# Two unused strips in SBUF that shift the start of nearly every tile in a partition

## The chip, the cores and the metric

The kernel runs on one core of one Trainium2 chip. The metric is the device time of one execution in microseconds (us); less is better. TensorE does the matrix products, ScalarE (ACT) and VectorE (DVE) everything elementwise, and the tiles that they share lie in SBUF, a memory of 128 partitions. A tile has an address inside a partition, the same in all 128; that address is what this change is about.

## What is computed

The reference is a two-layer encoder trunk on x of 256 tokens x 1024 channels, in float32. Each layer is: half a SwiGLU feed-forward network (FFN), a token mixer, half an FFN; the first layer's mixer is a gated linear attention (GLA) in both directions, the second's a differential softmax attention.

```
def swiglu_ffn(h, w_gu, w_down):
    gate, up = jnp.split(h @ w_gu, 2, axis=-1)
    return (jax.nn.silu(gate) * up) @ w_down
...
for i in range(DEPTH):
    x = x + 0.5 * swiglu_ffn(rms_norm(x, norm_g[i, 0]), ffn_w_gu[i, 0], ffn_w_down[i, 0])
    h = rms_norm(x, norm_g[i, 1])
    x = x + (gla_mixer(h, ...) if i % 2 == 0 else diff_mixer(h, ...))
    x = x + 0.5 * swiglu_ffn(rms_norm(x, norm_g[i, 2]), ffn_w_gu[i, 1], ffn_w_down[i, 1])
```

w_gu is 1024 x 5632, w_down 2816 x 1024; there are four FFNs, so most of the products are theirs.

## The kernel before

**Weights.** `weight_plan` lists all weights in the order of use, in pieces of at most 1024 rows x 256 columns. Each piece is loaded into one of three `stage` buffers (8 KB of a partition), five pieces ahead, by DMAs on SP's queue (L119). ACT and DVE then split it into a high and a low part in float32r, the type that TensorE takes at one pass (L157, one of five `w` buffers of 16 KB). A float32 product is made of three float32r products: high.high, high.low, low.high.

**Products.** A matrix product takes a stationary operand of 128 x 128, which a LDWEIGHTS (engine PEld in the profile) puts into the array, and a moving operand, whose columns stream past it. Three helpers issue nearly all of them:

- `mm3` (L181, L182) in the gate and up halves of the FFN (tiles ps_g, ps_u) and in its down half (ps_d): for each 128-deep slice one product of 512 moving columns (both parts of the activations against the high weights), and one of 256 (high activations against the low weights). Stationary: w. Moving: the normalised x (x2, shown as x) in gate and up, the gated activations a2 (shown as a) in down.
- `mm1` (L174 to L176): three products of 256 columns each; stationary w. Moving: x2 for GLA's q, k and low-rank products, and the mixers' normalised outputs (o of GLA, do of the differential mixer) in `out_proj` (ps_w).
- `project_tok` (L196 to L198) and, in the last FFN, `down_out` (L388 to L390): three products of 256 columns each; stationary x2 or a2, moving w.

The small products of the mixers (scores, transposes, products with v) are in float32 or float32r on tiles of their own pools.

**Order.** The FFN runs over 11 pairs of column groups (gate, then up), then over 4 column groups of down in three pieces of depth each. The mixers follow an order written out by hand. All tiles come from pools, and the framework works out the waits; nothing in the source names an address.

**Addresses.** Pools lie one behind the other in the order in which they are opened, tiles inside a pool in the order in which they are first asked for, each on a multiple of 32 bytes. `const` comes first (the identity and the triangle `cst`, and small parameters), then `stage`, `wpool`, `xpool` (x and x2), `ev`, `small` (the statistics, some 50 tiles of 8 to 512 bytes), and behind it the pools that are opened for one stage at a time. All tiles of `stage`, `wpool`, `xpool` and of the stages' pools are whole multiples of 512 bytes, but for a few, so one remainder holds for a whole pool. In the program as built, the first byte of a tile, modulo 512, is:

| tiles | before | after |
|---|---|---|
| cst (identity, triangle) | 128 | 224 |
| stage, w, x, x2, acc, sq, half, rb | 416 | 0 |
| small statistics | all multiples of 32 | all multiples of 32 |
| a2, gate, up, sg, GLA's qk, v_tm, o2, w2, lr, the differential mixer's qkn, dv_tm, dT, o2 | 192 | 0 |
| qkd (GLA's decayed q and k) | 320 | 128 |

Every operand slice of a product begins a whole multiple of 512 bytes behind its tile's first byte, so it has its tile's remainder.

Of the kernel before, what the change touches and what calls it, by code (L numbers as in the profile page):

```python
# [11 lines left out]
F32 = mybir.dt.float32  # L12
# [6 lines left out]
P = 128  # L19
T = 256  # L20
# [17 lines left out]
# the differential mixer: h half a projection; for pair of heads p: bp statistics, np normalized q and k,  # L38
# sph scores and softmax of head h, fp the transposed probabilities, ap their products with v, op normalized; hold keeps weights
# from being split  # L40
# [3 lines left out]
# the gated linear attention: h half a projection; z the gate's logits, y its log decay, pi prefix sums of pair of  # L44
# heads i, ri its scores before decay, d l t the next level's decays, scores and place among the scores,
# ai products with v, gi output gate, oi normalized; hold keeps weights from being split, x lets them go
# [8 lines left out]
def weight_plan(w):  # L55
    """The weights in the order of use: [rows, columns] pieces of at most 1024 x 256, slices of rows, columns, copies."""
    plan = []

    def cols(a, start, width=CW, times=1):
        plan.append((a[:, start : start + width], KD, width, times))  # L60

    def ffn(i, j):
        gu, down = w["ffn_w_gu"][i, j], w["ffn_w_down"][i, j]
        for c in range(FF // CW):
            cols(gu, c * CW)
            cols(gu, FF + c * CW)
        for dc in range(D // CW):
            for k0 in range(0, NFB, KD):
                n = min(KD, NFB - k0)
                plan.append((down[k0 * P : (k0 + n) * P, dc * CW : (dc + 1) * CW], n, CW, 1))  # L70

    ffn(0, 0)
    gla = w["gla_w_in"][0]
    # four times side by side, to have the ranks on four groups of partitions
    cols(gla, gla.shape[1] - 32, 32, 4)
    for kind, c in GLA_COLS.split():
        cols(gla, {"q": 0, "k": 512, "v": 1024, "g": 2048}[kind] + int(c) * CW)
    for c in range(4):
        cols(w["gla_w_out"][0], c * CW)
    ffn(0, 1)  # L80
    ffn(1, 0)
    for kind, c in DIFF_COLS.split():
        cols(w["diff_w_in"][0], "qkv".index(kind) * D + int(c) * CW)
    for c in range(4):
        cols(w["diff_w_out"][0], c * CW)
    ffn(1, 1)
    return plan
# [3 lines left out]
def trunk(ctx: ExitStack, tc: tile.TileContext, ins, out):  # L91
# [3 lines left out]
    const = ctx.enter_context(tc.tile_pool(name="const", bufs=1))  # L95
    stage = ctx.enter_context(tc.tile_pool(name="stage", bufs=N_STAGE))
# [3 lines left out]
    small = ctx.enter_context(tc.tile_pool(name="small", bufs=2))  # L100
    psA = ctx.enter_context(tc.tile_pool(name="psA", bufs=6, space=bass.MemoryType.PSUM))
# [4 lines left out]
    plan = weight_plan(ins)  # L106
    staged, split = {}, {}
# [15 lines left out]
    def parts():  # L123
        """The parts of the next weights to split."""
        i = state["split"]
        _, nk, width, times = plan[i]
        t = staged.pop(i)
        w = split[i] = wpool.tile([P, KD, 2, CW], FR, tag="w", name=f"w{i}")
        state["split"] += 1
        step = 2 if i < 2 else 4  # L130
        for k0 in range(0, nk, step):
            ks = slice(k0, min(k0 + step, nk))
            whole, wh, wl = t[:, ks, :width], w[:, ks, 0, : times * width], w[:, ks, 1, : times * width]
            if times > 1:
                shape = [P, whole.shape[1], times, width]
                whole = whole[:, :, None, :].broadcast_to(shape)
                wh, wl = (z.rearrange("p k (c n) -> p k c n", c=times) for z in (wh, wl))
            high = partial(nc.scalar.activation, wh, whole, AF.Copy)
            low = partial(nc.vector.tensor_tensor, out=wl, in0=whole, in1=wh.bitcast(F32), op=ALU.subtract)
            yield high, low  # L140
# [10 lines left out]
    def issue(ops, after):  # L151
        """Each operation behind those of `after` that run on its engine."""
        with ExitStack() as order:
            for i in after:
                order.enter_context(tc.issue_after(i.ins))
            for op in ops:
                op()  # L157

    def release(*after):
        """The parts held back, behind `after`."""  # L160
        issue(held, after)
        held.clear()
        state["hold"] = None
# [8 lines left out]
    def mm1(ps, w, ms, act, k, first, last):  # L172
        """ps += wh.xh + wh.xl + wl.xh for one 128-deep slice."""
        mm(ps, lhsT=w[:, k, 0, ms], rhs=act[:, k, 0, :], start=first, stop=False)  # L174
        mm(ps, lhsT=w[:, k, 0, ms], rhs=act[:, k, 1, :], start=False, stop=False)  # L175
        mm(ps, lhsT=w[:, k, 1, ms], rhs=act[:, k, 0, :], start=False, stop=last)  # L176

    def mm3(ps, w, ms, act, k, first, last, wk=None):
        """ps[:, 0:256] += wh.xh + wl.xh, ps[:, 256:512] += wh.xl for one 128-deep slice."""
        wk = k if wk is None else wk  # L180
        mm(ps, lhsT=w[:, wk, 0, ms], rhs=act[:, k, :, :], start=first, stop=False)  # L181
        mm(ps[:, 0:T], lhsT=w[:, wk, 1, ms], rhs=act[:, k, 0, :], start=False, stop=last)  # L182
# [18 lines left out]
    def join(banks, out_t):  # L201
        """out = both halves of three-pass products."""
        h = ev.tile([P, 2, T], F32, tag="half", name="half")
        for b, ps in enumerate(banks):
            nc.scalar.copy(h[:, b, :], ps[:, T:512])  # L205
            nc.vector.tensor_tensor(out=out_t[:, b, :], in0=ps[:, 0:T], in1=h[:, b, :], op=ALU.add)  # L206

    def rsqrt(v, shape, name):
        """v ** -0.5 for v > 0."""
# [22 lines left out]
    # the tensor engine runs at half its clock until it has been busy for a while  # L232
# [18 lines left out]
    def load_gate(w2):  # L251
        """The second gate weights as rows of high, low, high, low parts, zero against the other direction's ranks."""
# [54 lines left out]
    def down(act, nk, coef, norm):  # L307
        """x += coef * act @ w, and the next norm's blocks as they come."""
# [26 lines left out]
    def out_proj(act, norm, parts, late):  # L335
        """x += act @ w; the two first column groups wait for `late` with their last slices."""
# [28 lines left out]
    def by_token(xt):  # L365
        """x with the tokens on the partitions."""
# [10 lines left out]
    def down_out(act, nk, coef, xt):  # L377
        """out = x + coef * act @ w, with the tokens on the partitions."""
# [18 lines left out]
    def first_norm():  # L397
        n = Norm(0)
        with ExitStack() as xctx:
# [8 lines left out]
            # neighbouring blocks lie in different banks, so that two engines can follow each other  # L408
# [73 lines left out]
    def gla(norm, nxt, w2):  # L482
        QK = KD // 2
        with ExitStack() as gctx:
# [7 lines left out]
            with tc.tile_pool(name="glb", bufs=2) as lp:  # L492
                # gate path: low rank -> log decay -> prefix sums per tile of 128 tokens
# [6 lines left out]
                # both directions' ranks, twice the high parts, twice the low ones  # L500
# [8 lines left out]
                def project_half(kind, c, n):  # L509
                    """Half a column group: of q and k half the columns, of v and g half the tokens."""  # L510
# [21 lines left out]
                # sums before each token, per pair of heads: forward's from column 0, backward's from column 1  # L532
# [5 lines left out]
                def gate_logits():  # L538
                    """z and exp(-|z|)."""
# [22 lines left out]
                def scores(q, k, name, cross=False):  # L562
                    """Scores^T [j, tile, head, i] of two heads."""
# [7 lines left out]
                def decay(hp, level):  # L571
                    """exp of the decays of queries and keys to the level's boundaries."""
# [14 lines left out]
                    if s == 1:  # L587
                        # the keys lie next to their boundary
# [130 lines left out]
    # relative-position bias by distance: frel[h, t] = table[bucket(t - 255), h]  # L719
# [14 lines left out]
    def diff(norm, nxt):  # L734
        with ExitStack() as octx:
            dp = octx.enter_context(tc.tile_pool(name="dif", bufs=1))
            # lambda
# [23 lines left out]
            def project_half(key, t, done):  # L761
                """Half the tokens of a column group; `done` takes the whole."""
                if t == 0:
                    half[key] = next_weights(), psA.tile([P, 2, CW], F32, tag="A", name="ps_d{}{}{}".format(*key))
                w, ps = half[key]
                project_tok(w, norm.x2, None, ps, (t,))
                if t == 1:
                    done(ps)
# [15 lines left out]
            def qk_stats(hp):  # L784
                # bias[q, k] with the queries in reverse: frel[h, k + (255 - q)]
# [4 lines left out]
                # mean square of q and k plus eps over the squared norm of x  # L790
# [24 lines left out]
            def softmax(hp, b):  # L815
# [22 lines left out]
                # p1 - lambda p2 times the sum of the first softmax, which the norm takes out again  # L838
# [28 lines left out]
            def attend(c):  # L867
                """Heads 2c and 2c + 1."""
# [31 lines left out]
            # halves of projections (h) between the steps of the pairs of heads  # L900
# [28 lines left out]
def constants():  # L929
    """What depends on the shapes alone."""  # L930
# [39 lines left out]
```

## Time and profile before

| | us |
|---|---|
| time, median of three runs | 1002.21 |
| lowest, highest run | 1001.0, 1005.1 |
| span of the profiled execution, first to last instruction | 1000.1 |
| PE busy in it | 994.5 |
| DVE, ACT busy in it | 748.0, 567.7 |

The profiled execution is one run with the hardware profiler; its span leaves out what lies before the first and behind the last instruction. A busy PE is not a PE at its best pace: a product counts as busy from its start to its modelled end, and products overlap. The pace is seen in the distance between the starts of two products.

### The profile page before, as it was taken

What the parts mean: (1) busy time and instruction counts of PE and PEld (TensorE: products, weight loads), DVE (VectorE), ACT (ScalarE), POOL (GpSimd) and SP (SyncE); (2) the same over time, 40 slices, a digit from 0 to 9 for tenths busy, and PEclk for the clock granted to TensorE, in tenths of its full rate; (3) what the DMA queues carried; (4) which work ended last, traced back from release to release, by engine and by line L of the source; (5) the groups of instructions that cost most, each with busy time, mean ns of one, the idle gap of its engine ahead of it and who ended that gap; (6) DMA issues with size and microseconds to landing.
All of it is one profiled execution on the core that took longest, in us unless ns stands there. A gap on an engine that the chain in (4) does not pass through costs nothing.

```text
span 1000.1 us, 16172 instructions
## 1 busy us (share of the span) xinstructions
PE 994.5 (99%) x6524; PEld 906.6 (91%) x6524; DVE 748.0 (75%) x1284; ACT 567.7 (57%) x962; POOL 2.0 (0%) x10
## 2 busy tenths in 40 slices
PE   9999999999999999999999999999999999999998
PEld 8888888999999888888888888889999998888998
DVE  6998756499877987774679787656989699767640
ACT  7666535397756755643456555435576577555430
POOL 0000000000000000000000000000000000000000
PEclk9999999999999999999999999999999999999999
DMA  9676544574322775545557555375655268555440
GB/s 295 221 263 209 190 158 135 194 226 154 127 85 85 256 248 178 190 159 187 167 176 248 195 184 178 128 240 171 194 149 169 65 200 274 178 171 193 158 132 22
DMA packets 176968, 178.95 MB, mean 179 GB/s; under 512 B 4419, under 2 KB 176222, under 8 KB 176894
## 3 DMA queue, kind: packets, MB, share of 16 engines
q1 hardware_dynamic: 176606, 177.68, 54.3%
q8 instruction: 51, 0.84, 0.3%
q10 hardware_dynamic: 256, 0.21, 0.1%
q14 instruction: 23, 0.19, 0.1%
q0 software_dynamic: 32, 0.02, 0.0%
HBM read 176.84 MB, written 1.06 MB: 178 GB/s over the span
## 4 chain that ended last, share of the span: by engine, by line
PE 98%; DVE 1%; DMA 0%; ACT 0%; issue 0%; ACTq 0%; POOLq 0%
PE ps_g L181 16%; PE ps_u L181 16%; PE ps_d L181 12%; PE ps_g L182 8%; PE ps_u L182 8%; PE ps_d L182 6%; PE ps_d L388 2%; PE ps_d L389 2%; PE ps_d L390 2%; PE ps_s L567 2%; PE ps_dqk L196 2%; PE ps_dqk L198 2%; PE ps_dqk L197 2%; PE ps_w L174 1%; PE ps_w L176 1%; PE ps_w L175 1%
## 5 line engine op out<-in xcount | busy, mean ns | idle before, releaser
L157 DVE TENSOR_TENSOR w<-stage,w 128x1024 fp32r<-128x1024 f32 x334 | 385.4, 1191 | 32.2 <-ACT w L157 31.9
L157 ACT ACTIVATE w<-stage 128x1024 fp32r<-128x1024 f32 x334 | 327.3, 1030 | 45.4 <-PE ps_d L390 17.0
L181 PE MATMUL ps_g<-x,w 128*128 128x512 f32 x704 | 249.3, 397 | 0.0
L181 PE MATMUL ps_u<-x,w 128*128 128x512 f32 x704 | 248.7, 395 | 0.0
L182 PE MATMUL ps_u<-x,w 128*128 128x256 f32 x704 | 197.5, 281 | 0.0
L182 PE MATMUL ps_g<-x,w 128*128 128x256 f32 x704 | 197.1, 281 | 0.0
L181 PE MATMUL ps_d<-a,w 128*128 128x512 f32 x528 | 183.2, 390 | 0.0
L181 PEld LDWEIGHTS ps_g<-x,w 128*128 128x128 f32 x704 | 132.0, 188 | 31.0 <-issue 0.9
L181 PEld LDWEIGHTS ps_u<-x,w 128*128 128x128 f32 x704 | 132.0, 188 | 30.7
L182 PE MATMUL ps_d<-a,w 128*128 128x256 f32 x528 | 149.0, 282 | 0.0
L182 PEld LDWEIGHTS ps_g<-x,w 128*128 128x128 f32 x704 | 133.4, 189 | 0.5
L182 PEld LDWEIGHTS ps_u<-x,w 128*128 128x128 f32 x704 | 133.1, 189 | 0.1
L181 PEld LDWEIGHTS ps_d<-a,w 128*128 128x128 f32 x528 | 99.1, 188 | 20.7
L182 PEld LDWEIGHTS ps_d<-a,w 128*128 128x128 f32 x528 | 99.9, 189 | 0.0
L276 ACT ACTIVATE x<-x,par 128x256 fp32r<-128x256 f32 x40 | 20.0, 507 | 117.5 <-DVE x L325 117.5
L205 ACT COPY half<-ps_u 128x256 f32<-128x256 f32 x88 | 32.7, 371 | 87.2 <-PE ps_u L182 85.4
L205 ACT COPY half<-ps_g 128x256 f32<-128x256 f32 x88 | 32.3, 370 | 83.5 <-PE ps_g L182 81.4
L206 DVE TENSOR_TENSOR up<-ps_u,half 128x256 f32<-128x256 f32 x88 | 36.9, 422 | 38.7 <-ACT half L205 38.6
L206 DVE TENSOR_TENSOR gate<-ps_g,half 128x256 f32<-128x256 f32 x88 | 36.8, 422 | 36.9 <-ACT half L205 36.9
L325 DVE SCALAR_TENSOR_TENSOR x<-ps_d,x 128x256 f32<-128x256 f32 x48 | 20.3, 424 | 57.9 <-PE ps_d L182 56.7
L388 PE MATMUL ps_d<-w,a 128*128 128x256 f32 x176 | 49.5, 281 | 0.0
L389 PE MATMUL ps_d<-w,a 128*128 128x256 f32 x176 | 49.5, 281 | 0.0
(232 smaller groups left out, 1560.6 us busy)
## 6 DMA issues: line engine op xcount, KB each, us to landing
stage<-in_ffn_w_gu_dram SPq DMA_DIRECT2D x86, 1024.0 KB, 5.1
stage<-in_ffn_w_down_dram SPq DMA_DIRECT2D x32, 1024.0 KB, 4.8
stage<-in_ffn_w_down_dram SPq DMA_DIRECT2D x16, 768.0 KB, 4.1
stage<-in_gla_w_in_dram SPq DMA_DIRECT2D x12, 1024.0 KB, 5.6
stage<-in_diff_w_in_dram SPq DMA_DIRECT2D x12, 1024.0 KB, 5.5
stage<-in_gla_w_out_dram SPq DMA_DIRECT2D x4, 1024.0 KB
stage<-in_diff_w_out_dram SPq DMA_DIRECT2D x4, 1024.0 KB, 4.9
stage<-in_ffn_w_gu_dram SPq DMA_DIRECT2D x8, 256.0 KB, 5.7
```

Of the source, the lines that this page charges most:

```text
L157: op()
L181: mm(ps, lhsT=w[:, wk, 0, ms], rhs=act[:, k, :, :], start=first, stop=False)
L182: mm(ps[:, 0:T], lhsT=w[:, wk, 1, ms], rhs=act[:, k, 0, :], start=False, stop=last)
L196: mm(ps[:, t, :], lhsT=act[:, k, 0, ts_], rhs=w[:, k, 0, :], start=k == 0, stop=False)
L197: mm(ps[:, t, :], lhsT=act[:, k, 0, ts_], rhs=w[:, k, 1, :], start=False, stop=False)
L198: mm(ps[:, t, :], lhsT=act[:, k, 1, ts_], rhs=w[:, k, 0, :], start=False, stop=k == KD - 1)
L205: nc.scalar.copy(h[:, b, :], ps[:, T:512])
L206: nc.vector.tensor_tensor(out=out_t[:, b, :], in0=ps[:, 0:T], in1=h[:, b, :], op=ALU.add)
L325: nc.vector.scalar_tensor_tensor(out=x[:, d, :], in0=ps[:, h * T : (h + 1) * T], scalar=coef, in1=x[:, d, :], op0=ALU.mult, op1=ALU.add,)
L388: mm(ps, lhsT=act[:, k0 + k, 0, ts_], rhs=w[:, k, 0, :], start=first, stop=False)
L389: mm(ps, lhsT=act[:, k0 + k, 0, ts_], rhs=w[:, k, 1, :], start=False, stop=False)
L390: mm(ps, lhsT=act[:, k0 + k, 1, ts_], rhs=w[:, k, 0, :], start=False, stop=last)
```

## The change

Two tiles are asked for that nothing writes or reads: 96 bytes of each partition at the front of `const`, and 224 bytes at the end of what `small` has asked for at that point. They shift what lies behind them; the table above has both states. Nothing else changes but comments and docstrings, which are gone: with the line numbers left out, the built program has the same instructions on the same engines in the same order, with the same waits, row for row. Lines behind L95 stand three lines further down in the changed kernel (L181 becomes L184).

```
     const = ctx.enter_context(tc.tile_pool(name="const", bufs=1))
+
+    const.tile([P, 24], F32, name="gap0")
     stage = ctx.enter_context(tc.tile_pool(name="stage", bufs=N_STAGE))
     wpool = ctx.enter_context(tc.tile_pool(name="wpool", bufs=N_W))
     xpool = ctx.enter_context(tc.tile_pool(name="xpool", bufs=1))
     ev = ctx.enter_context(tc.tile_pool(name="ev", bufs=2))
     small = ctx.enter_context(tc.tile_pool(name="small", bufs=2))
+    small.tile([P, 56], F32, tag="gap", name="gap1", bufs=1)
     psA = ctx.enter_context(tc.tile_pool(name="psA", bufs=6, space=bass.MemoryType.PSUM))
```

The 224 bytes bring the stages' pools, and the 96 bytes those ahead of `small`, to multiples of 512.

## Rows read from the trace of the kernel before

**Rows 1.** Page: busy us of each engine; granted TensorE clock; the chain by engine.
```profile
PE 994.5 (99%) x6524; PEld 906.6 (91%) x6524; DVE 748.0 (75%) x1284; ACT 567.7 (57%) x962; POOL 2.0 (0%) x10
...
PEclk9999999999999999999999999999999999999999
...
PE 98%; DVE 1%; DMA 0%; ACT 0%; issue 0%; ACTq 0%; POOLq 0%
```

**Rows 2.** Groups by line: count, busy us, mean ns of one, idle before.
```profile
L181 PE MATMUL ps_g<-x,w 128*128 128x512 f32 x704 | 249.3, 397 | 0.0
...
L181 PE MATMUL ps_d<-a,w 128*128 128x512 f32 x528 | 183.2, 390 | 0.0
...
L388 PE MATMUL ps_d<-w,a 128*128 128x256 f32 x176 | 49.5, 281 | 0.0
...
L196 PE MATMUL ps_dqk<-w,x 128*128 128x256 f32 x128 | 36.6, 286 | 0.0
```

**Rows 3.** PE in order of time, first FFN's gate and up, 60 to 80: first, last of 117.
```profile
59.68 0.39 PE L181 MATMUL ps_g<-x,w 128*128 128x512 f32 x1
...
79.79 0.39 PE L181 MATMUL ps_g<-x,w 128*128 128x512 f32 x1
```

**Rows 4.** As rows 3, second FFN's gate and up, 400 to 420: first, last of 115.
```profile
399.79 0.28 PE L182 MATMUL ps_g<-x,w 128*128 128x256 f32 x1
...
419.93 0.28 PE L182 MATMUL ps_u<-x,w 128*128 128x256 f32 x1
```

**Rows 5.** Stretches: busy us of PE (instructions), granted clock, DMA share, GB/s.
```profile
550.00:570.00 20.00, 20.00 (x117) 1.00 0.60 200
840.00:860.00 20.00, 20.00 (x115) 1.00 0.71 236
```

**Rows 6.** As rows 3, second FFN's down, 460 to 480: first, last of 117.
```profile
459.68 0.39 PE L181 MATMUL ps_d<-a,w 128*128 128x512 f32 x1
...
479.79 0.39 PE L181 MATMUL ps_d<-a,w 128*128 128x512 f32 x1
```

**Rows 7.** As rows 3, differential mixer's q and k, 697 to 712: first, last of 128.
```profile
696.74 0.28 PE L196 MATMUL ps_dqk<-w,x 128*128 128x256 f32 x1
...
711.98 0.28 PE L197 MATMUL ps_dqk<-w,x 128*128 128x256 f32 x1
```

**Rows 8.** As rows 3, GLA's output projection, 306 to 319: first, last of 113.
```profile
305.82 0.28 PE L175 MATMUL ps_w<-o,w 128*128 128x256 f32 x1
...
318.89 0.28 PE L176 MATMUL ps_w<-o,w 128*128 128x256 f32 x1
```

**Rows 9.** As rows 3, last FFN's down, 950 to 970: first, last of 172.
```profile
949.75 0.28 PE L390 MATMUL ps_d<-w,a 128*128 128x256 f32 x1
...
969.99 0.28 PE L390 MATMUL ps_d<-w,a 128*128 128x256 f32 x1
```

**Rows 10.** Pieces of the chain: start us, us, what (mixers' small products).
```profile
202.41 0.92 PE ps_z L543 x4
...
289.27 0.43 PE ps_av L635 x2
...
785.76 1.80 PE ps_do L874 x16
```

**Rows 11.** Groups by line and shape: DVE and ACT at 512 elements.
```profile
L472 DVE TENSOR_TENSOR a<-up,a 128x512 fp32r<-128x512 f32 x44 | 30.2, 686 | 0.8 <-ACT a L471 0.7
L471 ACT ACTIVATE a<-up 128x512 fp32r<-128x512 f32 x44 | 27.5, 624 | 2.2 <-DVE up L469 2.1
...
L157 DVE TENSOR_TENSOR w<-stage,w 128x512 fp32r<-128x512 f32 x18 | 12.2, 685 | 0.0
...
L157 ACT ACTIVATE w<-stage 128x512 fp32r<-128x512 f32 x18 | 11.0, 616 | 0.0
```

**Rows 12.** Page: DMA queue of the weights; SP's longest wait by line.
```profile
q1 hardware_dynamic: 176606, 177.68, 54.3%
...
SPq L119 <- DVE w L157: 783.0, 153, 19.4
```

More of the change, by code (lines that the diff above doesn't have):

```diff
@@ L95, in trunk @@
     const = ctx.enter_context(tc.tile_pool(name="const", bufs=1))
+    const.tile([P, 24], F32, name="gap0")
     stage = ctx.enter_context(tc.tile_pool(name="stage", bufs=N_STAGE))
@@ L100, in trunk @@
     small = ctx.enter_context(tc.tile_pool(name="small", bufs=2))
+    small.tile([P, 56], F32, tag="gap", name="gap1", bufs=1)
     psA = ctx.enter_context(tc.tile_pool(name="psA", bufs=6, space=bass.MemoryType.PSUM))
```

## The prediction

> **What bounds the kernel now.** I read the page first. [...] The groups of PE show no idle time ahead of them [rows 2]. So there is no wait to shorten: the time is the sum of the distances between the starts of 6524 products, and a change moves it through that pace or hardly at all. I therefore took the timeline of PE in stretches where one pattern repeats, and divided: (start of the last row - start of the first) / steps between them. A "pair" is one product of 512 and one of 256 moving columns of `mm3`.
>
> - First FFN, gate and up: 59.68 to 79.79 in 116 steps, 58 pairs: 346.7 ns a pair [rows 3].
> - Second FFN, the same code on the same addresses modulo 512: 399.79 to 419.93 in 57 pairs: 353.3 ns [rows 4]. The third FFN has 117 rows in 20 us as the first, the fourth 115 as the second [rows 5].
> - Down: 459.68 to 479.79 in 58 pairs: 346.7 ns [rows 6].
> - Differential mixer's q and k, 256 columns each: 15.24 us in 127 steps: 120.0 ns [rows 7].
> - GLA's output projection, 256 columns each: 13.07 us in 112 steps: 116.7 ns [rows 8].
> - Last FFN's down, 256 columns each: 20.24 us in 171 steps: 118.4 ns [rows 9].
>
> The reader is to see two things. The pace has two levels that differ by 2 to 3%: quick (346.7, 116.7) and slow (353.3, 120.0). And the level goes with the remainders of the two operands. Written as (moving, stationary): (416, 416) gives 120.0 at 256 columns, and either 346.7 or 353.3 in pairs; (192, 416) gives 116.7 and 346.7; (416, 192) gives 118.4. 416 is an odd multiple of 32, 192 is a multiple of 64. The slow pace is at its fullest where both operands begin at an odd multiple of 32, and it is absent where the moving one does not.
>
> **The change part by part.** It adds no instruction and no wait and takes none away; the order on each engine is the same. What can change is the duration of what reads and writes the shifted tiles.
>
> *DVE and ACT.* The same shape at two remainders: at 512 elements DVE takes 686 ns on tiles at 192 and 685 ns on tiles at 416, ACT 624 and 616 [rows 11]. No price of the remainder shows up to multiples of 64, so I take 0. If something smaller came of it, PE's idle column of 0.0 covers it [rows 2]: neither engine is waited for in the steady stretches.
>
> *DMA.* The weights' rows now land at 0 instead of 416. Their queue keeps the 16 engines busy for 54.3% of the span, and SP's queue spends 783.0 us waiting for DVE to free a stage buffer [rows 12], so a load that ends sooner only waits longer. I take 0. The one load that PE itself waits for is in the first 10 us, worth some tenths of a us either way.
>
> *Transposes.* cst goes from 128 to 224, an odd multiple of 32. It is the moving operand of the transposes and of GLA's prefix sums, 160 instructions. At the 3.3 ns that separate the two paces of 256 columns this is 0.5 us at most (no row has cst elsewhere): 0 to +0.5, and I take 0.
>
> *The products.* Now every large operand pair is (0, 0). I take for it the quick pace, since 0 is a multiple of 64, as 192 is:
> (a) gate and up of the FFNs that run slow. The second and the fourth do [rows 4, 5]; each has 11 x 2 x 16 = 352 pairs (ps_g and ps_u have 704 products of 512 columns each over four FFNs [rows 2]): 2 x 352 x 6.6 ns = 4.7 us.
> (b) 256 columns at (416, 416): L196 to L198 with 128 + 64 + 64 + 64 products each, L174 to L176 with 72 each that have x2 as moving operand: 3 x (320 + 72) = 1176, x 3.3 ns = 3.9 us.
> (c) the last down: 3 x 176 = 528 [rows 2], x 1.7 ns = 0.9 us.
> (d) down (1056 products) and the output projections (384) are at the quick pace already: 0.
> The sum is 9.5 us. The profiled span of 1000.1 becomes 990.6. The median of the runs is 2.1 us above that span, so 992.7, rounded to **993**.
>
> The bounds of (a) to (d) from other rows: no gain at all, if the remainder has nothing to do with the pace; and the paces of the small float32 products as a floor. Those run at 112 ns with 128 columns (1.80 us for 16), and at 216 ns with one float32 pass over 256 (0.43 us for 2) [rows 10], which I take as the nearest rows for 256 and 512 float32r columns. They give the third rival below.
>
> [...]
>
> **The rivals.**
>
> *The remainder does nothing.* The two paces would be states into which the stream of products falls at the start of a stretch, and the mixers' difference would come from what precedes them. For it: the first and the second FFN have the same remainders and different paces, so the remainder alone doesn't decide. Against it: q, k, v, g and the differential mixer's q, k, v come to 120.0 after every interruption, some 30 times, and the output projections to 116.7 to 118 each time. Time: 1002.2, with 352 x 6.6 ns = 2.3 us for each gate-and-up stage that changes its state: 998 to 1007. The three runs of before lie 4.1 us apart, about two such steps.
>
> *Slower: equal remainders are what is slow.* The rows allow the other reading: (416, 416) is slow because the two are equal, so that the two streams of reads keep step, and (192, 416) and (416, 192) are quicker because they differ. After the change all are equal. Down may fall to the slow pace, 528 x 6.6 = 3.5 us; the output projections 384 x 3.3 = 1.3; the last down 528 x 1.6 = 0.8: +5.6 us, 1007.8. If the quick gate-and-up stages go slow as well, +4.7 more, 1012.5; if down stays quick, 1004.3. What decides is whether down after the change runs at 346.7 or 353.3. For it: four float32r products of GLA's gate, 512 columns at (192, 192), take 0.92 us, 230 each [rows 10], no quicker than the 512-column products of the FFN; so being at multiples of 64 on both sides gives nothing beyond the quick pace, and perhaps not even that. Against it: in the first FFN (416, 416) runs at 346.7.
> [...]
>
> *Larger gain.* Even the quick pace is above the floor: 346.7 against 216 + 112 = 328. If a start at a multiple of 128 or 512, which no large operand of before has, removes that too, the pairs give 18.7 ns on 704 + 528, and 25.3 on 704: 23.0 + 17.8; 256 columns give 8.0 on 1176, 4.7 on 384 and 6.4 on 528: 9.4 + 1.8 + 3.4. In all 55 us: 947; half of it: 974. For it: nothing in the trace excludes it. Against it: the pace is the same 346.7 at 416 and at 192, where some difference would be expected, and GLA's 230 ns.
>
> **How the numbers follow.** Quick pace everywhere 0.36 (its own range 988 to 998), the remainder does nothing 0.30, equal remainders 0.20, larger gain 0.14. A difference of 0.5%, 5 us, is about what a measurement of this kernel can tell from none: 997.2 and 1007.2 are the bounds. Faster: 0.31 + 0.14 + 0.01 = 0.46. Slower: 0.15 of the equal remainders and 0.02 of the stages' states: 0.17. Same: 0.37. The range goes up to the middle of the equal remainders, 1008, and down to a little beyond half the larger gain, 970; outside are about 0.06 above and 0.10 below.
>
> **What would show it.** In the changed kernel's timeline: 346.7 ns a pair in all four gate-and-up stages (117 rows in 20 us, never 115); 116.7 instead of 120.0 in the differential mixer's q and k; 116.7 in the last down; down and output projections unchanged. Mean durations of L181 with x as moving operand would be near 390 ns as those of down are, not 397 [rows 2]. It is wrong if q and k stay at 120.0 (the remainder does nothing, or equality is what counts), if down or the output projections slow down (equality), or if any pair goes below 340 ns (larger gain).

## The result: slower, and the profile after

| | before | after |
|---|---|---|
| median, us (6 runs each) | 1002.88 | 1010.41 |
| lowest, highest | 1000.46, 1005.1 | 1008.87, 1011.04 |
| span of the profiled execution | 1000.1 | 1008.6 |

The ratio of after to before is 1.0079, with a 95% interval of 1.0063 to 1.0094: about 8 us slower, where 993 us had been forecast, outside the range of 970 to 1008.

The page of the changed kernel has the same shape as that of before [rows 1]; PE is still the bound, and its busy time has grown with the span:

```profile
PE 1003.1 (99%) x6524; PEld 908.2 (90%) x6524; DVE 748.4 (74%) x1284; ACT 568.3 (56%) x962; POOL 2.0 (0%) x10
...
PEclk9999999999999999999999999999999999999999
```

DVE and ACT moved by 0.4 and 0.6 us, the granted clock not at all (9 in all 40 slices of both pages). In the groups by line (mean ns of one behind the busy time) the product that has changed most is the one that was to stay as it was: the 512-column product of down, 390 ns before [rows 2], has 399 now, as gate has.

```profile
L184 PE MATMUL ps_g<-x,w 128*128 128x512 f32 x704 | 251.0, 399 | 0.0
...
L184 PE MATMUL ps_d<-a,w 128*128 128x512 f32 x528 | 186.7, 399 | 0.0
```

The timeline of PE, in the second FFN's down (465 to 485, 115 rows), GLA's output projection (311 to 323, 103 rows) and the last FFN's down (960 to 980, 169 rows), first and last row of each:

```profile
464.77 0.28 PE L185 MATMUL ps_d<-a,w 128*128 128x256 f32 x1
...
484.91 0.28 PE L185 MATMUL ps_d<-a,w 128*128 128x256 f32 x1
```

```profile
310.75 0.28 PE L179 MATMUL ps_w<-o,w 128*128 128x256 f32 x1
...
322.99 0.29 PE L179 MATMUL ps_w<-o,w 128*128 128x256 f32 x1
```

```profile
959.81 0.28 PE L391 MATMUL ps_d<-w,a 128*128 128x256 f32 x1
...
979.97 0.28 PE L391 MATMUL ps_d<-w,a 128*128 128x256 f32 x1
```

The time from the first start to the last, divided by the steps between them: 20.14 us in 57 pairs, 353.3 ns (before 346.7 [rows 6]); 12.24 us in 102 steps, 120.0 ns (116.7 [rows 8]); 20.16 us in 168 steps, 120.0 ns (118.4 [rows 9]). The differential mixer's q and k stay at 120.0 [rows 7]. In gate and up, stretches of 20 us (and one of 16) show 115 products where the pace is 353.3 and 117 where it is 346.7:

```profile
60.00:80.00 20.00, 20.00 (x115) 1.00 0.79 256
...
560.00:580.00 20.00, 20.00 (x115) 1.00 0.54 177
840.00:860.00 20.00, 20.00 (x115) 1.00 0.80 261
914.00:930.00 16.00, 16.00 (x94) 1.00 0.54 178
```

The third FFN and, from 45 us on, the first, both quick before [rows 3, 5], are slow now. The fourth begins slow, as before, but from its interruption by the transposes of x on (895 to 899 us) it is quick: 353.3 from 828 to 895 us, 346.7 from 899 us on (94 in 16 us).

The 8.5 us of the span can be given to stages: the first product of each stage starts, in the two timelines, at these times.

| stage | start before | start after | longer by |
|---|---|---|---|
| first FFN, gate and up | 8.96 | 8.89 | 1.75 |
| down | 134.21 | 135.89 | 1.17 |
| GLA | 195.23 | 198.08 | 0.55 |
| second FFN, gate and up | 319.71 | 323.11 | 0.10 |
| down | 444.77 | 448.27 | 1.17 |
| third FFN, gate and up | 505.79 | 510.46 | 2.13 |
| down | 628.82 | 635.62 | 1.17 |
| differential mixer | 689.84 | 697.81 | 0.40 |
| fourth FFN, gate and up | 807.16 | 815.53 | -0.80 |
| last down | 934.25 | 941.82 | 0.9 |

Of the last column (a stage's length after less its length before) the three downs make 3.5 us, gate and up 3.2, the two mixers 0.95, the last down 0.9. No stage of any length became quicker but a part of the fourth gate and up. The last down's 0.9 counts to the end of the span.

### The profile page after: what moved, and what is told of

The parts are those of the page before. It is cut to its first block, busy times and chain, and to the rows that moved or that the text cites. A ratio compares the mean times of both kernels' runs of the same rounds, so it can differ in the third digit from the quotient of the medians.

```text
span 1008.6 us, 16172 instructions
## 1 busy us (share of the span) xinstructions
PE 1003.1 (99%) x6524; PEld 908.2 (90%) x6524; DVE 748.4 (74%) x1284; ACT 568.3 (56%) x962; POOL 2.0 (0%) x10
## 3 DMA queue, kind: packets, MB, share of 16 engines
q1 hardware_dynamic: 176606, 177.68, 53.3%
## 4 chain that ended last, share of the span: by engine, by line
PE 98%; DVE 1%; DMA 0%; ACT 0%; issue 0%; ACTq 0%; POOLq 0%
PE ps_g L184 16%; PE ps_u L184 16%; PE ps_d L184 12%; PE ps_g L185 8%; PE ps_u L185 8%; PE ps_d L185 6%; PE ps_d L393 2%; PE ps_d L392 2%; PE ps_d L391 2%; PE ps_s L570 2%; PE ps_dqk L199 2%; PE ps_dqk L201 2%; PE ps_dqk L200 2%; PE ps_w L177 1%; PE ps_w L178 1%; PE ps_w L179 1%
## 5 line engine op out<-in xcount | busy, mean ns | idle before, releaser
L184 PE MATMUL ps_g<-x,w 128*128 128x512 f32 x704 | 251.0, 399 | 0.0
L184 PE MATMUL ps_u<-x,w 128*128 128x512 f32 x704 | 250.2, 398 | 0.0
L184 PE MATMUL ps_d<-a,w 128*128 128x512 f32 x528 | 186.7, 399 | 0.0
L184 PEld LDWEIGHTS ps_g<-x,w 128*128 128x128 f32 x704 | 132.3, 188 | 32.5 <-issue 0.9
L184 PEld LDWEIGHTS ps_u<-x,w 128*128 128x128 f32 x704 | 132.1, 188 | 32.1
L184 PEld LDWEIGHTS ps_d<-a,w 128*128 128x128 f32 x528 | 99.2, 188 | 24.7
```

## The experiments

The theory after the result: the pace of a stream of products hangs on the **distance** of its two operands, the moving one's address less the stationary one's, and not on where each begins. Theory E below is its first form (equal remainders are what is slow), theory D its later one (only the distance modulo 256 bytes counts). The rival: it hangs on each operand's own remainder (theory O). All kernels below are the kernel before with strips in up to three places: `gap0` at the front of `const` (shifts everything behind it), `gapx` at the front of `xpool` (shifts x, x2 and what follows against w), `gap1` at the front of `small` (shifts the statistics and the stages' pools). Nothing else differs: the same instructions in the same order. Ratios are to the kernel before, run on the same chip.

**One strip alone.**

```
+    const.tile([P, 24], F32, name="gap0")
```

> Only the 96 bytes in const: w and x2 at 0 (equal), a2 and the mixers' outputs at 288, so that the distance of moving and stationary operand is that of before in every product. Theory E (equal remainders of the two operands are what is slow): down 346.7 ns a pair, output projections 116.7, last down 118.4, q and k of the differential mixer 120.0; time as before, 1000 to 1005. Theory O (an operand's own remainder counts; 0 and odd multiples of 32 are slow, 192 is quick): 288 is an odd multiple of 32, so down 353.3, output projections 120, as in the changed kernel; 1008 to 1011.

```
+    small.tile([P, 56], F32, tag="gap", name="gap1", bufs=1)
```

> Only 224 bytes in small: w and x2 stay at 416, a2 and the mixers' outputs come to 416 too, all equal but not at 0. Theory E: as the changed kernel: down 353.3 ns a pair, output projections 120, last down 120; 1007 to 1012. Theory O with 0 as what is slow: nothing is at 0, down stays at 346.7 and the time at 1000 to 1005. Theory O with odd multiples of 32 as what is slow: as theory E.

Measured: with the first strip alone 1005.03 us (1002.97 to 1006.49), ratio 1.0019 [1.0004, 1.0033]; with the second alone 1012.38 us (two runs, 1011.89 and 1012.86), ratio 1.0094 [1.0065, 1.0123]. The times lie a little above theory E's ranges, on a chip where the kernel before has a median of 1003.35. Second FFN's gate and up and its down, first with the first strip alone, then with the second alone (busy us, products, clock, DMA):

```profile
410.00:430.00 20.00, 20.00 (x115) 1.00 0.47 154
465.00:485.00 20.00, 20.00 (x117) 1.00 0.46 156
```

```profile
410.00:430.00 20.00, 20.00 (x115) 1.00 0.60 196
465.00:485.00 20.00, 20.00 (x115) 1.00 0.45 145
```

With w and x2 at 0 and a2 at 288, down is at 346.7 ns a pair (20.11 us in 58 pairs) as before; with everything at 416, it is at 353.3 (20.14 in 57) as in the changed kernel. So 0 is not what is slow (it is absent in the second kernel), and an odd multiple of 32 is not either (288 is one, and is quick): theory O falls in both its forms. The second strip makes the loss; the first is worth 0.2% (0.0 to 0.3), and its profiled span is 1.0 us longer than that of the kernel before (1001.1 and 1000.1). What the second strip does to down, the output projections and the last down follows from the distance of a2 and the mixers' outputs to w. With it the first and third FFN's gate and up are at 353.3 too, as in the changed kernel, though their own distance is 0 with the strip and without it; why is open.

**Other distances: 64 and 32, 256 and 128.**

```
+    const.tile([P, 24], F32, name="gap0")
...
+    xpool.tile([P, 64], F32, tag="gapx", name="gapx")
...
+    small.tile([P, 24], F32, tag="gap", name="gap1", bufs=1)
```

> w at 0, x2 at 256, a2 and the mixers' outputs at 128. Theory E with 512 as the modulus: no pair of operands is equal, so all pairs at 346.7 ns, 256 columns at 116.7 to 118.4; 994 to 998. With 256 as the modulus: x2 and w count as equal, gate and up, q and k as in the changed kernel (353.3, 120), down and the output projections quick; 1000 to 1006. With 128 or less: all slow, 1008 to 1011. Theory O with 0 modulo 128 as what is slow: all slow, 1008 to 1011.

```
+    const.tile([P, 24], F32, name="gap0")
...
+    xpool.tile([P, 16], F32, tag="gapx", name="gapx")
...
+    small.tile([P, 48], F32, tag="gap", name="gap1", bufs=1)
```

> w at 0, x2 at 64, a2 and the mixers' outputs at 32. Theory E with a modulus of 128 or more: no pair is equal, all pairs at 346.7 ns; 994 to 998. With 64 as the modulus: gate and up, q and k as in the changed kernel, down and the output projections quick; 1000 to 1006. With 32: all slow, 1008 to 1011. Theory O (0 and odd multiples of 32 slow): all slow but x2; 1004 to 1011.

Measured: 1007.26 us (three runs, 1007.04 to 1009.54), ratio 1.0045 [1.0019, 1.0072], and 1003.04 us (1000.41 to 1005.33), ratio 0.9998 [0.9979, 1.0016]. First the second FFN's gate and up with x2 256 away from w, then its down with a2 32 away:

```profile
410.00:430.00 20.00, 20.00 (x115) 1.00 0.59 196
```

```profile
465.00:485.00 20.00, 20.00 (x117) 1.00 0.63 209
```

With x2 256 away from w, gate and up of the first, second and third FFN are at 353.3 (115 products from 60 to 80, 410 to 430 and 560 to 580 us), and the fourth's at 346.7 (117 from 840 to 860): the two paces that equal remainders have. With a2 at distance 32, down is at 346.7, the output projection at 116.7 and the last down at 118.4: what the kernel before has at distance 288. So 256 counts as 0 here and 288 as 32; theory D takes the distance modulo 256 from these two. Neither theory had what the other distances gave; for the two kernels theory E, with a modulus of 256, had 1000 to 1006 and 994 to 998. At 128 down has a pace between the two (e3, 465 to 485, 57 pairs in 20.01 us: 351.1 ns), and at 64 gate and up are at 353.3 in some stretches (115 rows from 410 to 430, 560 to 580 and 840 to 860 us) and at 348.9 in the last stretch of the fourth (93 rows from 914 to 930 us). Quick or slow is not one switch: 351.1 and 348.9 lie between 346.7 and 353.3.

**The remaining distances.**

```
+    const.tile([P, 24], F32, name="gap0")
...
+    xpool.tile([P, 24], F32, tag="gapx", name="gapx")
...
+    small.tile([P, 80], F32, tag="gap", name="gap1", bufs=1)
```

> w at 0, x2 at 96, a2 and the mixers' outputs at 192: distances not seen yet. Theory D fixes what was seen: the last down has distance -192, that is 64, so 117.4 ns as GLA's q and k had at 64; output projections at 192, so 114 to 116 as the differential mixer's q and k had there. New: pairs at 96 and 192, 256 columns at 96 and 160; between 346 and 353 and between 114 and 120. Theory O or a modulus of 512 gives no reason why the last down should be at 117.4.

```
+    const.tile([P, 24], F32, name="gap0")
...
+    xpool.tile([P, 40], F32, tag="gapx", name="gapx")
...
+    small.tile([P, 72], F32, tag="gap", name="gap1", bufs=1)
```

> w at 0, x2 at 160, a2 and the mixers' outputs at 224. Theory D fixes: output projections at distance 224, so 118.3 ns as the last down had there; last down at distance -224, that is 32, so 116.9. New: pairs at 160 and 224, 256 columns at 160 and 96, which must be those of the kernel with x2 at 96, exchanged. Theory O gives 120 for the output projections (224 is an odd multiple of 32) and for the last down.

Measured: 1005.06 us (1002.68 to 1006.25), ratio 1.0012 [0.9999, 1.0024], and 1001.87 us (999.83 to 1003.75), ratio 0.9982 [0.9972, 0.9992]. What theory D fixed ahead came out within 0.4 ns in the one kernel (last down 117.8 for 117.4) and within 0.2 in the other (output projection 118.3 for 118.3, last down 116.7 for 116.9). The first of the two kernels also speaks against any form of theory O: a2 lies at 192 in it, as in the kernel before, but w at 0 instead of 416, and down is at 353.3 where it was at 346.7. The second FFN's down in it:

```profile
465.00:485.00 20.00, 20.00 (x115) 1.00 0.43 146
```

At distance 192 products of 256 columns have two paces. The output projection, from 310 to 319 us, is at 117.7, above the 114 to 116 that had been expected. Parts of the mixers' products with w moving in the kernel with x2 at 64, whose distance is 192 too, are at 113.3, and others of those at 117.8 (698 to 710 us). In that kernel, first and last of 47 rows, 5.21 us in 46 steps:

```profile
724.74 0.28 PE L199 MATMUL ps_dqk<-w,x 128*128 128x256 f32 x1
...
729.95 0.28 PE L200 MATMUL ps_dqk<-w,x 128*128 128x256 f32 x1
```

With all runs together, from stretches of 9 to 20 us as in the prediction (the 113.3 from shorter ones), ns:

| distance modulo 256 | pair of 512 and 256 columns | 256 columns |
|---|---|---|
| 0 | 353.3, in some stages 346.7 | 120.0 |
| 32 | 346.7 | 116.7 |
| 64 | 353.3, in one stretch 348.9 | 117.8 |
| 96 | 350.0 | 120.0 |
| 128 | 351.1 | 118.6 |
| 160 | 346.7 | 118.6 |
| 192 | 353.3 | 117.7, in some stretches 113.3 |
| 224 | 353.3 | 118.4 |

**The versions that follow from it.** Where x2 or a2 is moving and w stationary, the distance should be 32 by the table (346.7 and 116.7); the products with w moving then have 224 (118.4). Both kernels below have that, one with w at 416 and one with w at 0.

```
+    xpool.tile([P, 72], F32, tag="gapx", name="gapx")
...
+    small.tile([P, 56], F32, tag="gap", name="gap1", bufs=1)
```

> w stays at 416 as before, x2 and a2 both at 192. Theory D (only the distance moving minus stationary modulo 256 counts): distance 32 in gate, up, down, q, k and output projections, 224 in the products with x2 or a2 stationary. So gate and up 346.7 ns a pair in all four FFNs, q and k of GLA 116.9, the differential mixer's q and k 118.3, down and the rest as before: 4.7 + 0.6 + 1.4 us less than before where two gate-and-up stages are slow, 995 to 998. Rival S (gate and up fall into a state at their start whatever the distance): two or three of the four stages slow still, 999 to 1004.

```
+    const.tile([P, 24], F32, name="gap0")
...
+    xpool.tile([P, 8], F32, tag="gapx", name="gapx")
...
+    small.tile([P, 56], F32, tag="gap", name="gap1", bufs=1)
```

> The changed kernel with a third strip of 32 bytes ahead of x and x2: w stays at 0, x2 and a2 come to 32. Theory D: the same distances as with w at 416 and x2 and a2 at 192, so the same paces and the same time within 2 us, 995 to 998, some 13 us less than the changed kernel. Theory O (an operand's own remainder): w at 0 and the others at an odd multiple of 32 remain slow, 1008 to 1011.

Measured: 997.62 us (997.16 to 998.45), ratio 0.9939 [0.9926, 0.9952], and 996.9 us (995.45 to 998.46), ratio 0.9933 [0.992, 0.9947]. The second is the changed kernel with 32 bytes more, ahead of x2 and of all that follows it, and is 13.5 us quicker than it by the medians, 14.6 by the ratios to the kernel before. PE in its page, and gate and up of all four FFNs:

```profile
PE 988.0 (99%) x6524; PEld 905.8 (91%) x6524; DVE 748.0 (75%) x1284; ACT 568.0 (57%) x962; POOL 2.0 (0%) x10
```

```profile
60.00:80.00 20.00, 20.00 (x117) 1.00 0.82 264
410.00:430.00 20.00, 20.00 (x117) 1.00 0.50 163
560.00:580.00 20.00, 20.00 (x117) 1.00 0.58 189
840.00:860.00 20.00, 20.00 (x117) 1.00 0.66 216
```

117 in every one, and 346.7 ns in all four stages of the first kernel's profile too: at distance 32 no stage of gate and up falls into the slow pace in either, so the rival S, that a stage falls into its state whatever the distance, is out. The two kernels, whose operands begin elsewhere but at the same distance, agree within 0.7 us, as theory D had it.

## Why the prediction was wrong, step by step

- **What bounds the kernel** was right [rows 1, 2]. Every us of the 8.5 lies in the pace of PE; DVE, ACT and the granted clock did not move, and the loads' share went from 54.3% [rows 12] to 53.3% of a longer span; PE waits for a load only at the start, 0.6 us (0.7 before).
- **The levels of the pace** were read rightly from the timeline, and the step from paces and counts to a time holds: down was to lose 528 x 6.6 ns = 3.5 us if it went slow, and lost 3 x 1.17; the last down 0.8, and lost 0.9. What was passed over is that the last down's 118.4 [rows 9] was a third level, at a third distance.
- **The step that failed** is the sentence "I take for it the quick pace, since 0 is a multiple of 64, as 192 is". The three combinations of remainders in the trace allowed two readings, each operand's own remainder or the relation of the two, and I took the first. The run with a2 at 288 and that with everything at 416 show the second. The terms (a) to (c), a gain of 9.5 us in all, were worked out from the wrong reading. For (a) and (b) the distance of x2 and w is 0 before and after, so nothing in the change makes them quicker: q and k stay at 120.0, and gate and up lose 3.2 us in all instead of gaining 4.7. For (c) it went from 224 to 0, a loss of 0.9 instead of a gain of 0.9. Term (d), taken as 0, holds the largest part of the loss: 3.5 in the downs, which went from distance 32 to 0, and the mixers' 0.95, whose output projections did the same.
- **The rival "equal remainders"** was the right reading for the downs, the output projections and the last down, at 0.20, with the place that decides (down at 353.3) and its price, 1007.8 us, or 1012.5 with the quick gate-and-up stages. Measured is 1010.41: part of those did go slow, 3.2 of the 4.7 us. Why they did, at a distance that had not changed, neither the rival nor the runs say. What the rival lacked besides is the modulus of 256, which no row of before could give, and that unequal distances have paces of their own (350.0 at 96, 351.1 at 128).
- **"The remainder does nothing"** fell: 32 bytes between w and the tiles x2 and a2 are worth 13.5 us here (1010.41 and 996.9 us), and down goes from 353.3 to 346.7 with them. Two paces at one distance, which it calls states, are seen at 0, 64 and 192.
- **How the distance acts** was not tried. That two streams of reads keep step, as the rival of equal remainders has it, is its author's conjecture and was not shown; what the runs show is the pace at each distance.
- **"Larger gain"** fell: no pair went below 346.7 ns, at multiples of 512 or anywhere else. Only products of 256 columns came near the 112 ns that it priced, 113.3 at distance 192.

Open is why a gate-and-up stage with distance 0 takes sometimes 346.7 and sometimes 353.3. The kernel before has the quick pace in the first and third FFN (from 46 to 134 and 518 to 628 us); the one with the first strip alone there (117 products from 60 to 80 us, 118 from 560 to 580) and in the fourth from 840 to 860 us (118), but not from 914 to 930 (353.5); the changed kernel from 31 to 44 us and at the end of the fourth. In the traces of before and after the pace changes at interruptions by small products and stays from there on (before, second FFN: 346.4 from 326 to 331 us, then four products of ps_r, then 353.3 from 332 to 444), so it looks like a state that the stream falls into; what picks it is not known, and with one profiled execution of each kernel it can't be said whether another would fall alike.

The spread of the runs is some 4 us before and 1 to 3 us in the two kernels whose stages are all quick, so these two paces are not all of it. A part may lie at the start: the profiled executions of those two kernels are 2.6 us apart (996.5 and 993.9), and in the longer one PE waits 2.2 us for the load of x:

```profile
PE ps_x L415 <- DMA x_tm<-in_x_dram: 2.2, 1, 2.2
```

The prediction had put that load at some tenths of a us. Between the two profiles of before and after it played no part, since neither shows this wait.

## What to carry to other kernels

Where TensorE is the bound, measure the time between the starts of two products in steady stretches, stage by stage; here PE waited 2.3 us in all before, and levels 2 to 3% apart (346.7 and 353.3, 116.7 and 120.0) were what was left to chase. Here an alignment had no worth of its own: what counted was the distance of the moving operand from the stationary one. Aligning all tiles alike gave every large product distance 0, where down has 353.3 instead of 346.7, and took 1010.41 us instead of 1002.88; 32 bytes between the pools took the loss back and more (996.9). Where a trace allows two readings of few combinations, price both alike, and look for the kernel that has the missing combination before a reading is taken.

## What was not expected of the hardware

In these ten kernels the pace of the large float32r products went with the address distance of their two operands: 113.3 to 120.0 ns for 256 columns, 346.7 to 353.3 ns for 512 and 256 together. Two distances 256 apart gave the same paces where both were run: 0 and 256 (353.3 or 346.7), 32 and 288 (346.7, and 116.7 for 256 columns). It is not symmetric (32: 346.7, 224: 353.3). In these traces a stream has two paces at three distances: 346.7 or 353.3 at 0, 348.9 or 353.3 at 64, and 113.3 or 117.7 for 256 columns at 192; at 0 it keeps one until small products interrupt it (318 pairs at 353.3 in the second FFN before, 318 at 346.7 in the third). GLA's four float32r gate products, at distance 0 before and after, take 0.92 us before [rows 10] and 0.93 after.
